# Gate blocks beside the SSD scans, the LRU branch's products beside the last GDN head, head states loaded a head ahead, adaLN row weights on ScalarE's queue

## The chip, the cores and the metric

The kernel runs on one core of one Trainium2 chip. The metric is the device time of a run in microseconds (us). The kernel before takes 3340.12 us, the median of three runs (3339.49 to 3342.93).

## What is computed

One layer of a diffusion backbone with 1024 tokens of width 1024. Only the part around the change is shown; after it come a hierarchical mixture of experts and a final norm.

```python
h_l = rmsnorm(x_l) * (1 + mod_l[1]) + mod_l[0]          # adaLN rows: mod = silu(c) @ w_mod + b_mod
parts = h_l @ w_in                                       # 93 column blocks: LRU, GDN, SSD inputs, gates
lru_l = lru_branch(...)                                  # gated linear recurrence
gdn_l = gdn_branch(...)                                  # gated DeltaNet, 8 heads, two directions
ssd_l = ssd_branch(...)                                  # Mamba-2 scan, 2 groups of 8 heads, two directions
gates = sigmoid(gate_pre).reshape(b, l, 3, 1024)
acc = 0.0
for k in range(3):
    acc = acc + gates[:, :, k] * (branches[k] @ w_branch[k])
x_l = x_l + mod_l[2] * (acc @ w_out)                     # rows mod[2..5] are made beside the merge
```

Every large product is made from fp32 operands that are split into a high and a low part, and adds three products: high by high, low by high, high by low.

## The kernel before, in words

**Blocks.** The weights of `w_in` come in 93 blocks of 128 columns. For each block `WBlocks.get` loads the raw weights with SyncE's queue (`raw<-in_w_in`), ScalarE makes the high part (`whi`), VectorE or GpSimd the low part (`wlo`), and `mmblock` issues 48 TensorE matmuls of 512 columns into a PSUM tile `pj`. The 24 products of the merge (`w_branch`) and the 8 of the output projection (`w_out`) have the same 48 matmuls. There are two `pj` tiles, so a block can start while the one before it is being read.

**Side tasks.** Everything else (convolutions, scans, norms, head chains) is written as Python generators in a list (`add`, `post`). `run` goes through a list of jobs; a job is a block or a callable. `mmblock` calls `tick` between matmul triples, and each tick moves every side task that its clock takes to be ready by one step. So the instruction order of each engine is fixed when the program is built, by the job list, the flags that tasks wait for (`wait`, `until`, `take`) and the builder's clock. Each engine then works strictly through its own order. All instructions are recorded on line 255, so they are told apart here by the names of their tiles.

**Stages.** The order of jobs is LRU (to about 640 us), the context part of GDN (to 754), SSD group 0 (blocks, then its scan to 929), SSD group 1 (blocks, then its scan to 1179), the SSD output gate blocks and norm (to 1248), eight GDN heads (to about 2050), the left-over gate blocks (to 2107), the merge (to 2422), the output projection, routing and the experts.

**Gate blocks.** 24 of the 93 blocks make the merge gates. They depend on nothing but `hl` (the split tokens), so `gate_jobs` can put them anywhere. `gate_done` turns each into two half tiles `gt` with ScalarE and stores them to DRAM (`gate`) with ScalarE's queue. The table `G` gives their places: 4 behind LRU, 6 in the GDN context part, 2, 2 and 0 behind the blocks of SSD group 0, of group 1 and of the SSD output, 1, 4 and 3 behind heads 5, 6 and 7, and the last 2 in the tail.

**The SSD scan.** `ssd_intra` works in rounds for one chunk and direction: GpSimd makes masks `gm`, TensorE sums them (`parg`), ScalarE takes the exponential (`L`), VectorE and ScalarE scale it by the head's scores (`t`), GpSimd and VectorE multiply (`L`), and TensorE applies it (`py`). `ssd_scan` carries the state `sst`: TensorE `pcs` and `pss`, VectorE `tm`, `sst` and `ya`, GpSimd `xd`. `ssd_final` does the norm and 32 transposes `pto`.

**GDN heads.** `gdn_head_ops` makes keys, queries and decays of a head; `gdn_chain` then carries two states `S` (one per direction) through eight steps, each `ch` matmuls, `w` and `S` on VectorE and scalings `k`, `ktg` on ScalarE. The start states are loaded from DRAM (`S<-sgd`) at the chain's start with ScalarE's queue. One more block per head, the output gate `GZ+h`, is kept in tile `gz`.

**Merge.** `merge` goes through the branches in the order LRU, SSD, GDN (`MERGE`), k = 0, 1, 2, and for each through eight products j. `stage_branch` and `stage` load a branch row block from DRAM (`st<-br`, two buffers) and split it into `bh` and `bl`. Each product needs its gate row back (`gt<-gate`); the first branch writes `acc`, the others add to it. At its side `mod_rows` (one generator step per tick) makes the four adaLN rows on VectorE: for each row eight loads `wr<-in_w_mod` of 512 KB, eight `macc` instructions and two `pmr` matmuls. `drain` finishes what is left of it before `out_proj`.

Of the kernel before, what the change touches and what calls it, by code (L numbers as in the profile page):

```python
# [11 lines left out]
F32 = mybir.dt.float32  # L12
# [4 lines left out]
ALU = mybir.AluOpType  # L17
# [4 lines left out]
P = 128  # L22
D = 1024
KT = D // P
SEQ = 1024
# [9 lines left out]
MERGE = (0, 2, 1)  # L35
# [102 lines left out]
ZP = 2  # L138
# [130 lines left out]
class Core:  # L269
    def __init__(self, tc, io, ctx):  # L270
        self.tc = tc
        self.clk = Clock()
        self.nc = Engines(self.clk, tc.nc)
        self.io = io
        self.ctx = ctx
        self.cnt = 0
        self.post = []
        self.flags = set()
        self.live = [0, 0]
        self.gates = 0  # L280

    def pool(self, name, bufs=1, **kw):
        return self.ctx.enter_context(self.clk.pool(self.tc, name=name, bufs=bufs, **kw))
# [152 lines left out]
    def mod_rows(self):  # L436

        nc = self.nc
        w_mod, b_mod = self.io["w_mod"], self.io["b_mod"]
        mp = self.mg  # L440
        one = mp.tile([P, 1], F32, name="one")
        nc.vector.memset(one, 1.0)

        def load(i):
            w = mp.tile([P, D], F32, tag="w", name="wr", bufs=3)
            c0 = 2048 + D * (i // KT)
            nc.sync.dma_start(out=w, in_=w_mod[i % KT * P:(i % KT + 1) * P, c0:c0 + D])
            return w
        q = deque([load(0), load(1)])
        for i in range(4 * KT):  # L450
            k = i % KT
            if i + 2 < 4 * KT:
                q.append(load(i + 2))
            w = q.popleft()
            a = self.act[:, k, 0:1]
            if k == 0:
                acc = mp.tile([P, D], F32, tag="macc", name="macc", bufs=1)
                nc.vector.tensor_scalar(out=acc, in0=w, scalar1=a, scalar2=None, op0=ALU.mult)
            else:
                nc.vector.scalar_tensor_tensor(out=acc, in0=w, scalar=a, in1=acc, op0=ALU.mult, op1=ALU.add)  # L460
            if q:
                self.clk.last = self.clk.ready[q[0].tensor.name]
            yield
            if k == KT - 1:
                r = i // KT
                b = mp.tile([1, D], F32, tag="b", name="mb")
                nc.sync.dma_start(out=b, in_=b_mod[:, 2048 + D * r:2048 + D * (r + 1)])
                for n0 in (0, 512):
                    ps = self.aux.tile([P, 512], F32, tag="aux", name="pmr")
                    nc.tensor.matmul(ps[0:1, :], lhsT=one, rhs=acc[:, n0:n0 + 512], start=True,  # L470
                                     stop=True)
                    nc.vector.tensor_tensor(out=b[:, n0:n0 + 512], in0=b[:, n0:n0 + 512], in1=ps[0:1, :], op=ALU.add)
                    yield
                nc.sync.dma_start(out=self.modrow[r:r + 1, :], in_=b)
# [991 lines left out]
    def gdn_head_ops(self, h, bts):  # L1466

        if h > 1:
            yield from self.wait(("gch", h - 2))
        yield from self.wait(("gpre", h))  # L1470
        for bt in bts:
            yield from self.gdn_keys(bt, norms=False)
        self.flags.add(("gkt", h))
        yield from self.wait(("gb", VB + h), *[("gop", 2 * h - 2, 1)] * (h > 0))
        for bt in bts:
            yield from self.gdn_values(bt)
        self.gd.used["vc"] -= 1
        yield from self.wait(*[("gi", bt.id) for bt in bts])
        for p in range(2):
            if h:  # L1480
                yield from self.wait(*([("gch", h - 1)] if p else [("gk3", h - 1)]))
            qs = [self.gd.tile([P, 4, P], F32, tag=f"qs{p}{d}", name="qs") for d in range(2)]
            e1 = self.e1d.rearrange("(t c) p -> t c p", c=16)
            for d in range(2):
                f = d if p == 0 else 1 - d
                self.nc.scalar.dma_start(out=qs[d], in_=e1[4 * f:4 * f + 4, 8 * d + h, :].unsqueeze(0).to_broadcast([P, 4, P]))
            yield
            for d in range(2):
                bt = bts[d if p == 0 else 1 - d]
# [92 lines left out]
    def gdn_chain(self, h, bts, og):  # L1582
# [2 lines left out]
        g = self.gd  # L1585
        if h > 1:
            yield from self.wait(("gch", h - 2))
        st = [g.tile([P, P], F32, tag="S", name="S") for _ in range(2)]
        for d in range(2):
            nc.scalar.dma_start(out=st[d], in_=self.sgd[h, d])  # L1590
        if h:
            yield from self.wait(("gch", h - 1))
        yield from self.wait(("gop", 2 * h, 0))
        pa, pb = self.ch
        for k in range(8):
# [80 lines left out]
    def gdn_jobs(self, n):  # L1676
# [31 lines left out]
            self.flags.add(("gpre", h))  # L1708

        def zdone(b, ps, lat):  # L1710
            if b > GZ and not LAZYZ:
                self.until(("gh", b - GZ - 1))
            self.add(zblock(b - GZ, ps))

        def zblock(h, ps):
            if h:
                yield from self.wait(("gh", h - 1))
            zs[h] = z = self.gd.tile([P, SEQ], F32, tag="gz", name="gz")
            self.nc.scalar.activation(out=z, in_=ps, func=AF.Silu)
            self.give(ps)  # L1720
            self.flags.add(("gz", h))
# [8 lines left out]
        jobs = blocks(0) + blocks(1) + self.gate_jobs(n[0])  # L1730
        for h in range(8):
            b = blocks(h + 2) if h < 6 else []
            jobs += [lambda h=h: head(h)] + b[:ZP] + [(GZ + h, "lat", zdone)] + b[ZP:]
            jobs += self.gate_jobs(n[1 + h])
        return jobs


    def split(self, hi, lo, src, scale=1.0):
# [25 lines left out]
    def merge(self, cur):  # L1764
        nc = self.nc
        mg = self.mg
        ma = self.ma
        acc = mg.tile([P, KT, SEQ], F32, tag="acc", name="acc", bufs=1)
        self.add(self.mod_rows())
        for k in range(3):  # L1770
            nx = []
            for j in range(KT):
                hi, lo = self.ws.get()
                gt = mg.tile([P, SEQ], F32, tag="gt", name="gt", bufs=2)
                nc.sync.dma_start(out=gt, in_=self.gate[8 * MERGE[k] + j])
                if k < 2 and j < 4:
                    nx.append(self.stage(mg, self.pair(ma, 12), self.br[MERGE[k + 1]][j]))
                ps = self.ppool.tile([P, SEQ], F32, tag="pj", name="pj")
                self.mmblock(ps, hi, lo, lambda i: cur[i], SEQ, self.tick, kouter=True)
                dst = acc[:, j, :] if k == 0 else gt  # L1780
                nc.vector.scalar_tensor_tensor(out=dst, in0=gt, scalar=1.0, in1=ps, op0=ALU.add, op1=ALU.mult)
                if k:
                    nc.vector.tensor_tensor(out=acc[:, j, :], in0=acc[:, j, :], in1=gt, op=ALU.add)
                if k == 2 and j < 4:
                    nx.append(self.pair(ma, 12))
                    self.split(nx[j][0], nx[j][1], acc[:, j, :], 0.5)
            for j in range(4, KT):
                if k < 2:
                    nx.append(self.stage(mg, self.pair(ma, 12), self.br[MERGE[k + 1]][j]))
                else:  # L1790
                    nx.append(self.pair(ma, 12))
                    self.split(nx[j][0], nx[j][1], acc[:, j, :], 0.5)
            cur = nx
        self.drain()
        return cur
# [488 lines left out]
def build(tc, io, out=None, stages=("lru", "ssd", "gdn", "moe"), dbg=None):  # L2284
    with ExitStack() as ctx:
        c = Core(tc, io, ctx)
        with tc.manual_schedule():
# [3 lines left out]
            c.gate = dr.tile([24, P, SEQ], F32, name="gate")  # L2291
            c.kvd = dr.tile([16, P, CTX], F32, name="kvd")
            c.e1d = dr.tile([P, P], F32, name="e1d")
            c.sgd = dr.tile([8, 2, P, P], F32, name="sgd")
            c.modrow = dr.tile([4, D], F32, name="modrow")
            c.x2d = dr.tile([SEQ, D], F32, name="x2d")
# [6 lines left out]
                dbg(c)  # L2303


G = {"mix": [0,1,2,2,2,2,2,2,2,2,2,2,2,2,1,0], "lru": 4, "gc": 6, "ssd": [2, 2, 0],
     "gdn": [0, 0, 0, 0, 0, 0, 1, 4, 3]}


def phase1(c, tc, io, stages):  # L2310
# [13 lines left out]
        J["ssd"] = c.ssd_jobs(0, G["ssd"][0]) + c.ssd_jobs(1, G["ssd"][1]) + c.gate_jobs(G["ssd"][2])  # L2324
    if "gdn" in stages:
        J["gdn"] = c.gdn_jobs(G["gdn"])
    J["tail"] = c.gate_jobs(24 - c.gates)
    order = [j for n in ("sm", "lru", "gc", "ssd", "gdn", "tail") for j in J[n] if not callable(j)]
    srcs = [io["w_in"][b] for b, _, _ in order]
    if "moe" in stages:  # L2330
# [2 lines left out]
    with c.clk.pool(tc, name="w", bufs=1, side="right") as c.wp, ExitStack() as psum, ExitStack() as right:  # L2333
        c.ppool = psum.enter_context(c.clk.pool(tc, name="pj", bufs=2, space=PSUM))
        c.aux = Banks(c, psum.enter_context(c.clk.pool(tc, name="aux", bufs=1, space=PSUM)), 4)
        with c.clk.pool(tc, name="hl", bufs=1) as hlp:
# [34 lines left out]
                c.ma = right.enter_context(c.clk.pool(tc, name="ma", bufs=1, side="right"))  # L2371
            with c.clk.pool(tc, name="gp", bufs=2) as c.gp, c.clk.pool(tc, name="st", bufs=1) as c.mg:
                cur = []
                if "moe" in stages:
                    c.add(c.stage_branch(0, cur))
                c.run(J["tail"])
                c.drain()
        if "moe" not in stages:
# [236 lines left out]
```

## Time and profile before

| what | value |
|---|---|
| median of 3 runs | 3340.12 us |
| profiled execution | 3341.23 us |
| its span | 3339.5 us |
| mean granted TensorE clock | 0.941 of full speed |
| TensorE matmuls busy | 2955.1 us, 88% |
| VectorE busy | 2141.1 us, 64% |
| ScalarE busy | 1573.0 us, 47% |
| GpSimd busy | 758.9 us, 23% |
| DMA, mean over the span | 129 GB/s |

A page of the profile gives shares over the whole span; the stages have different limits, so the views that matter here are cut to stretches of time. In them, PE is TensorE, PEld its weight loads, DVE is VectorE, ACT ScalarE, POOL GpSimd, SP SyncE, and a q behind an engine's name is its DMA queue. The granted clock is 1.00 at 2.4 GHz and falls towards 0.5 (1.2 GHz) in stretches where TensorE is throttled.

### The profile page before, as it was taken

The page shows a single profiled execution, that of the slowest core. Times are in us where ns is not written, and L with a number is a line of the kernel's source. Part 1 is how long each engine was busy: PE and PEld are TensorE (multiplying, and loading weights), DVE is VectorE, ACT ScalarE, POOL GpSimd, SP SyncE. Part 2 cuts the span into 40 slices and gives each one's busy share as a digit, 9 for nine tenths or more (in the row PEclk, how much of TensorE's full clock was granted, in tenths as well). Part 3 has the DMA queues.
Part 4 walks back from the last instruction along what each step waited for, and adds up shares of the span by engine and source line. Part 5 has one row for each costly group of instructions (what it writes and reads, how often), then busy time and mean ns, then how long its engine had stood idle before and what let it go on. Part 6 is the DMA issues. An engine that isn't in the chain of part 4 may idle for free. (4 is left out here: it accounts for less than half of the span.)

```text
span 3339.5 us, 47272 instructions
## 1 busy us (share of the span) xinstructions
PE 2955.1 (88%) x18539; PEld 2351.2 (70%) x18539; DVE 2141.1 (64%) x3730; ACT 1573.0 (47%) x2263; POOL 758.9 (23%) x642
## 2 busy tenths in 40 slices
PE   7978789989799789999999899889977899999992
PEld 3756667777478467787888777667765788878881
DVE  4677765744834836888788752244544888787785
ACT  4556564344225224455555443211122567676673
POOL 1121221203513512112021111211100233343333
PEclk9989999989799789999999999999988899999996
DMA  5112222211012011111121112455334698888895
GB/s 190 61 60 79 74 71 80 90 33 45 7 45 63 7 52 46 41 33 47 41 48 47 53 47 73 176 183 186 139 137 189 247 345 307 300 341 301 311 353 223
DMA packets 123009, 431.56 MB, mean 129 GB/s; under 512 B 18200, under 2 KB 44056, under 8 KB 97184
## 3 DMA queue, kind: packets, MB, share of 16 engines
q1 hardware_dynamic: 77712, 371.18, 31.0%
q10 hardware_dynamic: 33616, 36.34, 3.7%
q0 software_dynamic: 11456, 21.00, 1.8%
q8 instruction: 147, 2.41, 0.3%
q14 instruction: 78, 0.64, 0.1%
HBM read 389.57 MB, written 59.85 MB: 135 GB/s over the span
## 5 line engine op out<-in xcount | busy, mean ns | idle before, releaser
L255 PE MATMUL pj<-hhi,whi 128*128 128x512 f32 x1488 | 630.3, 424 | 10.1 <-DVE qT L255 5.0
L255 PE MATMUL pj<-hhi,wlo 128*128 128x512 f32 x1488 | 592.4, 398 | 3.7 <-POOL wlo L255 2.5
L255 PE MATMUL pj<-hlo,whi 128*128 128x512 f32 x1488 | 592.2, 398 | 0.0
L255 DVE TENSOR_TENSOR wl<-raw,wh 128x2048 fp32r<-128x2048 f32 x188 | 448.0, 2403 | 102.9 <-ACT wh L255 100.3
L255 POOL TENSOR_TENSOR wlo<-raw,whi 128x1024 fp32r<-128x1024 f32 x78 | 195.3, 2504 | 1027.3 <-ACT whi L255 911.5
L255 ACT ACTIVATE wh<-raw 128x2048 fp32r<-128x2048 f32 x188 | 360.6, 1918 | 128.7 <-PE psu L255 103.1
L255 PEld LDWEIGHTS pj<-hhi,wlo 128*128 128x128 f32 x1488 | 281.9, 189 | 74.1 <-POOL wlo L255 4.0
L255 PEld LDWEIGHTS pj<-hhi,whi 128*128 128x128 f32 x1488 | 283.7, 191 | 68.3 <-issue 6.8
L255 PEld LDWEIGHTS pj<-hlo,whi 128*128 128x128 f32 x1488 | 283.8, 191 | 56.3 <-issue 3.2
L255 ACT ACTIVATE whi<-raw 128x1024 fp32r<-128x1024 f32 x145 | 152.6, 1055 | 320.5 <-PE pj L255 233.0
L255 PE MATMUL psu<-wl,xh 128*128 128x512 f32 x576 | 227.4, 395 | 2.9 <-DVE wl L255 2.9
L255 PE MATMUL psu<-wh,xh 128*128 128x512 f32 x576 | 228.1, 396 | 0.0
L255 PE MATMUL psu<-wh,xl 128*128 128x512 f32 x576 | 226.1, 392 | 1.3 <-DVE xl L255 1.3
L255 DVE TENSOR_TENSOR wlo<-raw,whi 128x1024 fp32r<-128x1024 f32 x67 | 85.5, 1276 | 206.1 <-ACT whi L255 205.4
L255 ACT ACT_TABLE_LOAD x127 | 162.9, 1283 | 82.0 <-DVE xt L255 28.0
L255 POOL TENSOR_TENSOR yo<-yo,m 128x1024 f32<-128x1024 f32 x35 | 103.6, 2959 | 183.2 <-ACT yo L255 183.1
L255 PE MATMUL psg<-u,lw 128*128 128x512 f32 (+1 forms) x192 | 88.6, 598 | 56.2 <-issue 53.4
L255 PE MATMUL pj<-bh,whi 128*128 128x512 f32 x384 | 122.8, 401 | 14.6 <-DVE acc L255 8.7
L255 PEld LDWEIGHTS psu<-wl,xh 128*128 128x128 f32 x576 | 108.8, 189 | 29.8 <-DVE wl L255 8.3
L255 PE MATMUL pj<-bl,whi 128*128 128x512 f32 x384 | 122.1, 400 | 8.3 <-POOL bl L255 5.9
L255 PEld LDWEIGHTS psu<-wh,xl 128*128 128x128 f32 x576 | 108.7, 189 | 24.1 <-DVE xl L255 2.1
L255 PEld LDWEIGHTS psu<-wh,xh 128*128 128x128 f32 x576 | 109.2, 190 | 22.5 <-ACT xh L255 0.2
(472 smaller groups left out, 6189.0 us busy)
## 6 DMA issues: line engine op xcount, KB each, us to landing
raw<-in_w SPq DMA_DIRECT2D x188, 1024.0 KB, 7.4
raw<-in_w_in SPq DMA_DIRECT2D x119, 512.0 KB, 3.6
wr<-in_w_mod SPq DMA_DIRECT2D x32, 512.0 KB, 6.2
gate<-gt ACTq DMA_DIRECT2D x48, 256.0 KB, 2.0
raw<-in_w_branch SPq DMA_DIRECT2D x24, 512.0 KB, 3.6
st<-br SPq DMA_DIRECT2D x24, 512.0 KB, 4.8
gt<-gate SPq DMA_DIRECT2D x24, 512.0 KB, 5.0
wm<-in_w_mod SPq DMA_DIRECT2D x8, 1024.0 KB, 5.8
```

The costliest lines, as they stand in the source:

```text
L255: return f(*args, **kw)
```

## The change

It does five things. Ten gate blocks are put into the SSD stage (5, 4 and 1 in place of 2, 2 and 0), two each behind heads 5 and 6, none behind head 7 and none in the tail. The eight products of the merge's first branch leave the merge loop: six are made beside the chain of head 7 (`merge_jobs`, with operands that `merge_stage` writes over `hl`), two in the tail; each is scaled by its gate and stored to DRAM (`m0d`), and the merge loads the eight results into `acc` before its 16 remaining products. The block `GZ+7` stands before head 7 and uses a tile of tag `vc`. The states `S` are loaded by `gdn_head_ops` with SyncE's queue, one head ahead. And `mod_rows` issues its loads with ScalarE's queue in place of SyncE's.

```diff
@@ mod_rows
-            nc.sync.dma_start(out=w, in_=w_mod[i % KT * P:(i % KT + 1) * P, c0:c0 + D])
+            nc.scalar.dma_start(out=w, in_=w_mod[i % KT * P:(i % KT + 1) * P, c0:c0 + D])
@@ gdn_head_ops
+        bts[0].t["S"] = st = [self.gd.tile([P, P], F32, tag="S", name="S") for _ in range(2)]
+        for d in range(2):
+            self.nc.sync.dma_start(out=st[d], in_=self.sgd[h, d])
+        self.flags.add(("gs0", h))
         yield from self.wait(("gpre", h))
@@ gdn_chain
-        st = [g.tile([P, P], F32, tag="S", name="S") for _ in range(2)]
-        for d in range(2):
-            nc.scalar.dma_start(out=st[d], in_=self.sgd[h, d])
-        if h:
-            yield from self.wait(("gch", h - 1))
+        yield from self.wait(("gs0", h), *[("gch", h - 1)] * (h > 0))
+        st = bts[0].t["S"]
@@ gdn_jobs
-            if h:
+            if h == 7:
+                yield from self.take(self.gd, "vc")
+            elif h:
                 yield from self.wait(("gh", h - 1))
-            zs[h] = z = self.gd.tile([P, SEQ], F32, tag="gz", name="gz")
+            zs[h] = z = self.gd.tile([P, SEQ], F32, tag="vc" if h == 7 else "gz", name="gz")
...
+            if h == 6:
+                jobs.append(lambda: self.add(self.merge_stage(self.gd, "k")))
             jobs += self.gate_jobs(n[1 + h])
+            if h == 6:
+                jobs += [(GZ + 7, "lat", zdone), lambda: self.flags.add("hl"), lambda: head(7)]
+                jobs += self.merge_jobs(NM0, lambda: (self.gd, "k"))
+    def merge_stage(self, pool, tag):
+        def load(b):
+            raw = pool.tile([P, SEQ], F32, tag=tag, name="st")
+            self.nc.sync.dma_start(out=raw, in_=self.br[MERGE[0]][b])
+            return raw
+        yield from self.wait(("gkt", 7))
+        raw = [load(0), load(1)]
+        yield from self.wait("hl")
+        for b in range(KT):
+            self.split(self.hl[0][:, b, :], self.hl[1][:, b, :], raw[b])
+            if b + 2 < KT:
+                raw.append(load(b + 2))
+            self.flags.add(("mst", b))
+            yield
+        self.flags.add("mst")
+
+    def merge_jobs(self, n, where):
+        def job(j):
+            def rhs(i):
+                self.until(("mst", i))
+                return self.hl[0][:, i, :], self.hl[1][:, i, :]
+            hi, lo = self.ws.get()
+            while self.live[True] == 2:
+                self.tick(True)
+            self.live[True] += 1
+            ps = self.ppool.tile([P, SEQ], F32, tag="pj", name="pj")
+            self.mmblock(ps, hi, lo, rhs, SEQ, self.tick, kouter=not j)
+            self.add(done(j, ps))
+
+        def done(j, ps):
+            yield from self.wait("mst")
+            pool, tag = where()
+            gt = pool.tile([P, SEQ], F32, tag=tag, name="gt")
+            self.nc.sync.dma_start(out=gt, in_=self.gate[8 * MERGE[0] + j])
+            yield
+            self.nc.vector.scalar_tensor_tensor(out=gt, in0=gt, scalar=1.0, in1=ps, op0=ALU.add, op1=ALU.mult)
+            self.give(ps)
+            self.nc.sync.dma_start(out=self.m0[j], in_=gt)
+            yield
...
@@ merge
         self.add(self.mod_rows())
-        for k in range(3):
+        for j in range(KT):
+            nc.sync.dma_start(out=acc[:, j, :], in_=self.m0[j])
+        for k in range(1, 3):
...
-G = {..., "lru": 4, "gc": 6, "ssd": [2, 2, 0],
-     "gdn": [0, 0, 0, 0, 0, 0, 1, 4, 3]}
+G = {..., "lru": 4, "gc": 6, "ssd": [5, 4, 1],
+     "gdn": [0, 0, 0, 0, 0, 0, 2, 2, 0]}
+NM0 = 6
@@ phase1
-    J["tail"] = c.gate_jobs(24 - c.gates)
+    J["tail"] = c.merge_jobs(KT - c.merged, lambda: (c.mg, "gt"))
...
-                    c.add(c.stage_branch(0, cur))
+                c.add(c.stage_branch(1, cur))
```

TensorE does the same matmuls in both kernels, in another order.

**TensorE in the scan of SSD group 0.** Before, the second round of the scan stands alone; these rows follow the last block of the group:

```order
L255 MATMUL pcb<-cT,bT 128x128
L255 MATMUL pcs<-sst_178,cT 128x512
L255 MATMUL pcb<-cT,bT 128x128
L255 MATMUL pcs<-sst_179,cT 128x512
L255 MATMUL parg<-gm,mr 128x512 x4
L255 MATMUL pss<-xd,bt 128x512
L255 MATMUL parg<-gm,mr 128x512 x4
```

In the change the matmul triples of the added gate blocks stand between them:

```order
L255 MATMUL pcs<-sst_179,cT 128x512
L255 MATMUL pj<-hhi,whi 128x512
L255 MATMUL pj<-hlo,whi 128x512
L255 MATMUL pj<-hhi,wlo 128x512
L255 MATMUL parg<-gm,mr 128x512 x4
L255 MATMUL pcb<-cT,bT 128x128
L255 MATMUL pss<-xd,bt 128x512
L255 MATMUL pcs<-sst_180,cT 128x512
```

Three blocks that stood outside the scan of group 0 are spread over its rounds in this way, and two over those of group 1; the last four or five steps of each scan, which have no `parg`, still stand without blocks.

**SyncE's queue at the start of the merge.** Before, it loads the first branch and then one weight, one gate row, one row of the next branch and some `wr` per product:

```order
L255 DMA st<-br_77 128x1024
L255 DMA raw<-in_w_branch 128x1024
L255 DMA st<-br_77 128x1024 x7
L255 DMA raw<-in_w_branch 128x1024
L255 DMA gt<-gate 128x1024
L255 DMA st<-br_79 128x1024
L255 DMA wr<-in_w_mod 128x1024 x3
```

In the change these rows stand around the last products of the first branch and the first of the second:

```order
L255 DMA raw<-in_w_branch 128x1024
L255 DMA gt<-gate 128x1024
L255 DMA st<-br_79 128x1024
L255 DMA m0d<-gt 128x1024
L255 DMA gt<-gate 128x1024
L255 DMA st<-br_79 128x1024
L255 DMA m0d<-gt 128x1024
L255 DMA st<-br_79 128x1024 x4
L255 DMA acc<-m0d 128x1024 x8
L255 DMA raw<-in_w_branch 128x1024
L255 DMA gt<-gate 128x1024
L255 DMA st<-br_78 128x1024
```

The `wr` loads are gone from this queue, and the stores `m0d`, which wait for VectorE, and the eight loads of `acc` stand in it ahead of the rows of the second branch and of the weights.

**VectorE at the end of the merge.** Before, the last adaLN row is done some products earlier:

```order
L255 TENSOR_TENSOR mb<-mb,pmr 1x512
L255 SCALAR_TENSOR_TENSOR gt<-gt,pj 128x1024
L255 TENSOR_TENSOR acc<-acc,gt 128x1024
L255 SCALAR_TENSOR_TENSOR gt<-gt,pj 128x1024
L255 TENSOR_TENSOR acc<-acc,gt 128x1024
L255 TENSOR_TENSOR wlo<-raw,whi 128x1024
L255 SCALAR_TENSOR_TENSOR gt<-gt,pj 128x1024
L255 TENSOR_TENSOR acc<-acc,gt 128x1024
L255 SCALAR_TENSOR_TENSOR bl<-acc,bh 128x1024 x4
```

In the change it stands behind the last product:

```order
L255 SCALAR_TENSOR_TENSOR gt<-gt,pj 128x1024
L255 TENSOR_TENSOR acc<-acc,gt 128x1024
L255 SCALAR_TENSOR_TENSOR bl<-acc,bh 128x1024 x4
L255 TENSOR_TENSOR mb<-mb,pmr 1x512 x2
L255 TENSOR_SCALAR macc<-wr,act 128x1024
L255 SCALAR_TENSOR_TENSOR macc<-wr,act,macc 128x1024 x7
L255 TENSOR_TENSOR mb<-mb,pmr 1x512 x2
L255 TENSOR_TENSOR bl<-st,bh 128x1024 x4
```

The whole last row of `mod_rows` has moved behind the merge, where `drain` issues it before the output projection; on ScalarE's queue six of its eight loads stand ahead of the split of the next `w_out` weights.

## Rows read from the trace of the kernel before

**Rows 1.** The page, busy time of each engine: TensorE.
```profile
PE 2955.1 (88%) x18539; PEld 2351.2 (70%) x18539; DVE 2141.1 (64%) x3730; ACT 1573.0 (47%) x2263; POOL 758.9 (23%) x642
```

**Rows 2.** Stretches: length, busy PE, PEld, DVE, ACT, POOL (instructions); clock, DMA share, GB/s.
```profile
815.00:840.00 25.00, 24.43 (x120) 19.04 (x119) 20.17 (x41) 13.88 (x34) 15.07 (x20) 1.00 0.13 43
840.00:929.00 89.00, 63.92 (x198) 37.80 (x197) 72.41 (x122) 19.63 (x53) 49.98 (x59) 0.78 0.04 12
851.00:874.00 23.00, 17.10 (x60) 11.37 (x60) 17.71 (x34) 6.57 (x20) 14.51 (x20) 0.72 0.00 0
904.00:929.00 25.00, 18.10 (x41) 6.83 (x41) 24.00 (x34) 0.00 (x0) 10.75 (x7) 0.98 0.07 21
1092.00:1179.00 87.00, 63.39 (x197) 36.82 (x197) 71.84 (x121) 19.37 (x53) 49.14 (x58) 0.77 0.04 13
1228.00:1248.00 20.00, 9.23 (x43) 7.32 (x44) 6.68 (x13) 15.34 (x27) 0.00 (x0) 0.66 0.16 66
...
2049.00:2107.00 58.00, 58.00 (x263) 47.03 (x262) 7.39 (x14) 16.85 (x22) 9.61 (x4) 1.00 0.30 106
2107.00:2159.00 52.00, 40.17 (x148) 28.41 (x147) 14.94 (x12) 13.46 (x14) 14.37 (x6) 0.93 0.53 190
2159.00:2423.00 264.00, 245.88 (x1028) 190.67 (x1027) 124.53 (x96) 43.25 (x42) 41.51 (x17) 0.98 0.47 169
2423.00:2456.00 33.00, 18.11 (x51) 11.64 (x50) 13.54 (x10) 8.36 (x8) 8.14 (x3) 0.74 0.50 166
```

**Rows 3.** The same view for tile pj alone (block matmuls; no column for POOL).
```profile
815.00:840.00 25.00, 13.21 (x48) 8.66 (x48) 0.00 (x0) 1.20 (x2) 1.00 0.13 43
...
2015.00:2049.00 34.00, 15.50 (x50) 8.56 (x49) 0.00 (x0) 1.21 (x2) 0.95 0.12 39
2049.00:2107.00 58.00, 56.32 (x239) 44.16 (x238) 0.00 (x0) 5.79 (x9) 1.00 0.30 106
...
2159.00:2423.00 264.00, 237.87 (x1012) 189.99 (x1011) 26.05 (x22) 0.00 (x0) 0.98 0.47 169
```

**Rows 4.** Timeline of PE in the scan: start, length, instruction, [idle before <-releaser].
```profile
850.88 6.40 PE L255 MATMUL py<-xs,L 128*128 128x128 f32 x32 [2.89 <-POOL L L255]
...
898.04 6.70 PE L255 MATMUL py<-xs,L 128*128 128x128 f32 x32 [3.65 <-POOL L L255]
```

**Rows 5.** Timelines of DVE and POOL near 921 us, beside a block's low-part split.
```profile
921.07 0.68 DVE L255 TENSOR_TENSOR sst<-sst,pss 128x512 f32<-128x512 f32 x1
921.66 2.24 DVE L255 TENSOR_TENSOR ya<-ya,tm 128x512 f32<-128x512 f32 x1
...
920.56 2.79 POOL L255 TENSOR_TENSOR wlo<-raw,whi 128x1024 fp32r<-128x1024 f32 x1
```

**Rows 6.** Timelines of ACT, its queue and PE at the starts of two chains.
```profile
1908.06 0.91 ACTq L255 DMA_DIRECT2D S<-sgd  x2
1909.02 0.69 ACT L255 ACTIVATE k<-kt,ge 128x128 f32<-128x128 f32 x2
...
1915.64 1.22 PE L255 MATMUL ch<-S,WT 128*128 128x128 f32 x4 [9.58 <-DMA S<-sgd]
...
2020.47 1.22 PE L255 MATMUL ch<-S,WT 128*128 128x128 f32 x4 [4.86 <-DMA S<-sgd]
```

**Rows 7.** Timeline of SyncE's queue at the first products of the merge.
```profile
2103.85 20.89 SPq L255 DMA_DIRECT2D st<-br  x7
...
2158.09 11.00 SPq L255 DMA_DIRECT2D wr<-in_w_mod  x2
```

**Rows 8.** DMA issues of 2150 to 2400 us: KB each, median us to landing.
```profile
wr<-in_w_mod SPq DMA_DIRECT2D x27, 512.0 KB, 6.2
...
gt<-gate SPq DMA_DIRECT2D x20, 512.0 KB, 5.5
```

**Rows 9.** Groups of 2107 to 2423 us: busy us, mean ns | idle before <-releasers.
```profile
L255 DVE SCALAR_TENSOR_TENSOR macc<-wr,act,macc 128x1024 f32<-128x1024 f32 x28 | 44.3, 1584 | 10.1 <-DMA wr<-in_w_mod 9.6
...
L255 ACT ACTIVATE bh<-st 128x1024 fp32r<-128x1024 f32 x23 | 24.4, 1060 | 143.7 <-DMA st<-br 143.3 <-ACT gt L255 0.4
```

More of the change, by code (lines that the diff above doesn't have):

```diff
@@ L279, in __init__ @@
         self.live = [0, 0]
-        self.gates = 0
+        self.gates = self.merged = 0
     def pool(self, name, bufs=1, **kw):
@@ L1710, in zdone @@
         def zdone(b, ps, lat):
-            if b > GZ and not LAZYZ:
+            if GZ < b < GZ + 7:
                 self.until(("gh", b - GZ - 1))
@@ L1732, in gdn_jobs @@
             b = blocks(h + 2) if h < 6 else []
-            jobs += [lambda h=h: head(h)] + b[:ZP] + [(GZ + h, "lat", zdone)] + b[ZP:]
+            jobs += [lambda h=h: head(h)] * (h < 7) + b[:ZP] + [(GZ + h, "lat", zdone)] * (h < 7) + b[ZP:]
+            if h == 6:
+                jobs.append(lambda: self.add(self.merge_stage(self.gd, "k")))
             jobs += self.gate_jobs(n[1 + h])
-        return jobs
+            if h == 6:
+                jobs += [(GZ + 7, "lat", zdone), lambda: self.flags.add("hl"), lambda: head(7)]
+                jobs += self.merge_jobs(NM0, lambda: (self.gd, "k"))
+        return jobs
+    def merge_stage(self, pool, tag):
[35 more added lines that the diff above has]
+            yield
+        a = self.merged
+        self.merged += n
+        return [lambda j=j: job(j) for j in range(a, a + n)]
     def split(self, hi, lo, src, scale=1.0):
@@ L1779, in merge @@
                 self.mmblock(ps, hi, lo, lambda i: cur[i], SEQ, self.tick, kouter=True)
[L1780 to L1783, printed above, removed]
+                nc.vector.scalar_tensor_tensor(out=gt, in0=gt, scalar=1.0, in1=ps, op0=ALU.add, op1=ALU.mult)
+                nc.vector.tensor_tensor(out=acc[:, j, :], in0=acc[:, j, :], in1=gt, op=ALU.add)
                 if k == 2 and j < 4:
@@ L2293, in build @@
             c.e1d = dr.tile([P, P], F32, name="e1d")
+            c.m0 = dr.tile([KT, P, SEQ], F32, name="m0d")
             c.sgd = dr.tile([8, 2, P, P], F32, name="sgd")
@@ L2303, in build @@
                 dbg(c)
-G = {"mix": [0,1,2,2,2,2,2,2,2,2,2,2,2,2,1,0], "lru": 4, "gc": 6, "ssd": [2, 2, 0],
-     "gdn": [0, 0, 0, 0, 0, 0, 1, 4, 3]}
+G = {"mix": [0,1,2,2,2,2,2,2,2,2,2,2,2,2,1,0], "lru": 4, "gc": 6, "ssd": [5, 4, 1],
+     "gdn": [0, 0, 0, 0, 0, 0, 2, 2, 0]}
+NM0 = 6
 def phase1(c, tc, io, stages):
@@ L2326, in phase1 @@
         J["gdn"] = c.gdn_jobs(G["gdn"])
-    J["tail"] = c.gate_jobs(24 - c.gates)
+    assert c.gates == 24
+    J["tail"] = c.merge_jobs(KT - c.merged, lambda: (c.mg, "gt"))
     order = [j for n in ("sm", "lru", "gc", "ssd", "gdn", "tail") for j in J[n] if not callable(j)]
@@ L2373, in phase1 @@
                 cur = []
-                if "moe" in stages:
-                    c.add(c.stage_branch(0, cur))
+                c.add(c.stage_branch(1, cur))
                 c.run(J["tail"])
```

## The prediction

> **What bounds the kernel now.** I read the busy shares first: TensorE works 88% of the span [rows 1], and the change leaves its matmuls as they are. So only its idle time and its slow time can be won, and the next view is the one by stretches, which shows where these are. Three places matter. In the scans of the SSD groups (89 and 87 us) TensorE is busy about 63 us each, at a granted clock of 0.78 and 0.77 [rows 2], and the scan's last `py` and the one two rounds before it lie 47.2 us apart, with waits for GpSimd's `L` ahead of them [rows 4]: a round takes 23.6 us and its length is set by the loop over VectorE and GpSimd. In the end of the SSD stage (1228 to 1248) TensorE is busy 9.2 of 20 us. And around the merge it waits for operands: 40.2 of 52 us busy for the first three products, 18.1 of 33 in the entry to the output projection [rows 2]. The remaining stretch, 2049 to 2107, is full: five gate blocks, 239 block matmuls in 58 us, nearly all of it busy [rows 2, 3]. It gains nothing by being faster; it can only go elsewhere.
>
> **How the sum is made.** I count by marks in the profiled execution (3341.23 us, span 3339.5, 1.1 above the median). The heads 0 to 6 have the same number of blocks in both kernels: behind heads 5 and 6 one gate fewer, and `GZ+7` more. Six gate blocks more stand in the SSD stage, and what stood beside and behind head 7's chain is gone from there.
>
> **Removed.** From 2015 to 2107, in 34 + 58 = 92 us, lie `GZ+7` (50 block matmuls beside the chain) and five gate blocks [rows 3]. All six are now done earlier. That is −92 us, the one big term, and it is sure as far as the six blocks cost little in their new places and the chain finds other work beside it; both follow as terms.
>
> **SSD stage: +16 us.** A block is 48 matmuls of 512 columns; in the steady merge 1012 of them take 237.9 us [rows 3], 0.235 each, so a block is 11.3 us. In a round without a block TensorE works 17.1 of 23 us at a clock of 0.72 [rows 2], which is 12.3 us at full speed. 12.3 + 11.3 = 23.6: one block fills one round exactly. The block that already lies in the first round shows it: from 815 to 840 its 48 matmuls and 72 of the scan take 25 us, with TensorE busy 24.4 at full clock [rows 2, 3]; the scan alone does 60 in 23. So a block in a round costs between nothing and what is delayed when TensorE is full. Group 0 gets three blocks over about three rounds: 3 to 18 us, I take 10, nearer the middle because VectorE is nearly as full (72 of 89 us, and 24 of 25 in the last steps [rows 2]). Group 1 gets two, with one round that holds about 1.35: 0.35 × 11.3 = 4 us (0 to 9). The last one falls into the 20 us of the output norm, of which 10.8 are idle: 2 us (0 to 4). One GpSimd split beside the scan costs VectorE 2.24 instead of 0.68 us for an instruction that meets it, 1.6 us [rows 5]; two such splits, some 3 us, are in the 10 + 4. The Trainium skill (SBUF — State Buffer, the section on SBUF's two separate sides) says that GpSimd and VectorE share a port pair as an exclusive lock for a whole instruction. By that rule each split could hold VectorE for all its 2.79 us, 5.6 instead of 3 for two, and the sum would be 2 to 3 us higher; the one row here shows a part of that.
>
> **Head states: −8 us.** TensorE stands 9.6 and 4.9 us for `S`, whose loads were issued on ScalarE's queue a few us before [rows 6]. With the load a head ahead these waits end at the next latest thing: ScalarE's scaling `k` at 1909.0 to 1909.7, so about 6 of the first wait go, and of the second 1 to 3, where `k` follows the loads as closely. I take −8 (−3 to −12), since the clock also drops in such holes. The two loads go to SyncE's queue, where a 64 KB load ahead of 512 KB ones costs nothing that shows.
>
> **Chain and products: +6 us.** Before, 24 products take 52 + 264 = 316 us [rows 2]. Now: the chain of head 7 with product 0 beside it, 35 us (34 with one block before [rows 3]). Products 1 to 7 have operands and weights long ready: 7 × 11.3 = 79. Then the first three of the second branch. Before, the first branch was staged late: seven `st` loads took 20.9 us of SyncE's queue [rows 7], and three products took 52. In the change the `st` rows of the second branch stand in that queue behind the `m0d` stores, which wait for VectorE, and eight `acc` loads (4 MB) stand ahead of the next weights and gate rows. At best this hides beside products 6 and 7 (34 us), at worst it adds a landing of a gate row of 5.5 [rows 8] twice to the 52 (63). I take 52 again. The remaining 13 products: 264 us for 21.1 of them before, 12.5 each [rows 2, 3]. SyncE's queue then also held `wr` issues that waited up to 11.0 us for a buffer, ahead of the next weights [rows 7]; with them on ScalarE's queue I take 12.0, halfway to the 11.3 of full speed, 156 us. The danger is named below: ScalarE's own splits stand behind these waits now. In sum 35 + 79 + 52 + 156 = 322, against 316.
>
> **Entry to the output projection: +19 us.** `mod_rows` moves a step per tick, and 16 products give fewer ticks than 24. Its last row, eight `macc` of 1.27 us or more (mean 1.58 [rows 9]) with loads of 6.2 us [rows 8] and three buffers, now stands behind the last product. With two loads in and six to come, each about (6.2 + 1.3) / 3 = 2.5 us after the other, that is 15 us, and the `pmr` matmuls and the split of the `w_out` weights behind it some 4. VectorE is free of other work there, so nothing hides it: 33 us become 52. Bounds: 5, if the loads run ahead and half of the 8 × 1.27 = 10 us lies in the 15 us that the old entry stood idle anyway; and 30, if only two loads are under way at a time (3 × 7.5, and 8 behind it).
>
> **Sum.** −92 + 16 − 8 + 6 + 19 = −59: 3341.2 − 59 = 3282 us. ±0.2% is ±6.7 us, about what a measurement of this kernel can tell from no change.
>
> **Rivals.**
> 1. *The moved loads buy nothing.* The Trainium skill (DMA: Bandwidth & Descriptors, the section "Issuing engines are not separate DMA queues") says that transfers of all issuing engines run on the same 16 DMA engines. Without the gain in pitch the 13 products stay at 12.5: +7, 3289 us. The wait of `wr` issues in SyncE's queue [rows 7] speaks against it, the DMA share of 0.47 [rows 2] neither way. Chance 0.10.
> 2. *ScalarE's queue becomes the wait.* A `wr` load waits for a `macc` before it on VectorE, and ScalarE's `bh` and `whi` splits stand behind it. If each of 13 products loses 2.5 to 3 us by that, about half of a landing of 6.2 us [rows 8]: +33 to 40, 3315 to 3322 us. For it: 11 us long waits of `wr` before [rows 7]. Against: ScalarE is busy 43 of 264 us there [rows 2], and its `bh` instructions wait 143 us for `st` as it is [rows 9]. Chance 0.12.
> 3. *Blocks in the scan are only half hidden.* Five times 5.6 is 28 instead of 14, and with it the late staging (63) or the long entry (30) that go with a VectorE running late: +25 to +36, 3307 to 3318. For it: VectorE at 24 of 25 us [rows 2]. Chance 0.08.
> 4. *Slower: the scan's hops queue behind triples.* TensorE works in order. If a hop (`pcs`, `pss`, `parg`, `py`) is ready while three block matmuls (0.7 us) stand ahead of it, eight times in a round, and nothing is hidden, a block costs 11.3 + 5.6 = 16.9 us: five make 84 and the last 2, 86 instead of 16, 3352 us. It decides the sign when a round with a block takes over about 39 us, for the rest of the change is worth 75, 15 per block. Against: 815 to 840 with a block in it was no longer than a round alone [rows 2, 3]. Chance 0.03.
> 5. *Better.* Products and staging run at full speed: 13 at 11.3 (−9) and the first three hidden partly (−8 to −11): 3262 to 3266. Chance 0.09.
> 6. *The states come early but the chain still waits.* If it is `k`, behind `gt` and `whi` on ScalarE, that ends last, the −8 go: 3290. Chance 0.04.
>
> **How the numbers follow.** The forecast has 0.54; with its bounds (not all at one end) it spans 3266 to 3302. The range of 3260 to 3314 takes in rivals 1 and 6, most of 5 and about half of 2 and 3; outside lie some 0.17. Faster by over 0.2% has 0.94: all but rival 4 and the upper ends of 2 and 3 coming together, 0.03 for no change, 0.03 for slower.
>
> **What would show it.** Rounds of the SSD scans at 22 to 27 us and a granted clock near 1.0 in them; the scan of group 1 ending about 14 us later than before, near 1193; no TensorE idle of over 3 us ahead of `ch<-S,WT`; no stretch of gate blocks behind head 7; products 1 to 7 at 11.3 us; `pmr` and `macc` in a gap of some 50 us behind the last product. The forecast is wrong if rounds take over 35 us, if ScalarE's splits wait for its own `wr` issues in most products, or if the entry to the output projection is as short as before.

## The result, and the profile after

| | median us | range, runs | ratio to before, 95% interval |
|---|---|---|---|
| before | 3339.8 | 3336.1 to 3342.9, 4 | |
| the change | 3298.93 | 3295.62 to 3303.31, 4 | 0.9877 (0.9865 to 0.9890) |

The change is 41 us faster where 58 were forecast. The time lies in the range of 3260 to 3314, 17 us above the point. The profiled execution took 3298.6 us, its span is 3296.9. These lines of the page answer to [rows 1] and to the clock of 0.941:

```profile
span 3296.9 us, 47286 instructions
PE 2918.7 (89%) x18539; PEld 2331.5 (71%) x18539; DVE 2144.6 (65%) x3734; ACT 1569.8 (48%) x2260; POOL 756.0 (23%) x638
```

TensorE has as many instructions as before and is busy 36 us less, and the mean granted clock is 0.954 instead of 0.941: more of them ran at the upper level. Where the time went is read from the view by stretches of the changed kernel (length, busy PE, PEld, DVE, ACT, POOL; clock, DMA share, GB/s), against [rows 2]:

```profile
840.00:905.00 65.00, 61.33 (x284) 47.68 (x284) 48.20 (x80) 22.38 (x54) 46.14 (x53) 0.97 0.15 49
905.00:934.00 29.00, 20.89 (x55) 9.24 (x53) 24.55 (x39) 3.90 (x8) 10.22 (x8) 0.94 0.05 18
1099.00:1136.00 37.00, 34.57 (x161) 27.09 (x160) 28.64 (x48) 13.28 (x31) 23.09 (x30) 1.00 0.17 57
1136.00:1190.00 54.00, 39.27 (x132) 21.82 (x131) 42.81 (x72) 11.03 (x29) 26.66 (x29) 0.87 0.03 11
1250.00:1259.00 9.00, 5.89 (x34) 3.63 (x32) 4.42 (x8) 8.18 (x11) 0.00 (x0) 1.00 0.45 177
2001.00:2021.00 20.00, 15.96 (x86) 13.23 (x85) 3.17 (x6) 10.80 (x26) 1.62 (x1) 1.00 0.28 80
2021.00:2067.00 46.00, 29.77 (x177) 23.59 (x177) 19.31 (x44) 17.81 (x31) 13.84 (x20) 1.00 0.24 80
2067.00:2148.00 81.00, 79.02 (x342) 63.20 (x340) 19.69 (x22) 10.28 (x11) 7.21 (x3) 1.00 0.43 156
2148.00:2210.00 62.00, 43.55 (x145) 32.02 (x146) 18.37 (x15) 10.37 (x10) 11.88 (x5) 0.81 0.63 227
2210.00:2365.00 155.00, 148.55 (x633) 117.73 (x631) 85.75 (x65) 26.68 (x26) 22.24 (x9) 0.99 0.55 188
2365.00:2414.00 49.00, 20.70 (x58) 10.57 (x58) 24.87 (x22) 8.47 (x8) 7.96 (x3) 0.76 0.48 160
```

In order: the scan of SSD group 0 with its three blocks in it is nearly full at a clock of 0.97, and only its last steps (905 to 934) still leave TensorE idle. In the scan of group 1 the 37 us with its two blocks are full, the 54 behind them are not (busy 39.3, clock 0.87). The norm leaves 9 us where it left 20. `GZ+7` takes 20 us, the chain of head 7 with product 0 takes 46, products 1 to 7 take 81. The first three products of the second branch take 62 us, busy 44 of them; the other 13 take 155; and the entry to the output projection takes 49, busy 21. TensorE has idle time in three stretches behind 2021; what they cost against the old merge, which had idle time too, the experiments show.

### The profile page after: what moved, and what is told of

Its sections match the earlier page's. It is cut to its first block, busy times and chain, and to the rows that moved or that the text cites. A ratio compares the mean times of both kernels' runs of the same rounds, so it can differ in the third digit from the quotient of the medians.

```text
span 3296.9 us, 47286 instructions
## 1 busy us (share of the span) xinstructions
PE 2918.7 (89%) x18539; PEld 2331.5 (71%) x18539; DVE 2144.6 (65%) x3734; ACT 1569.8 (48%) x2260; POOL 756.0 (23%) x638
## 5 line engine op out<-in xcount | busy, mean ns | idle before, releaser
L255 PE MATMUL pj<-hhi,whi 128*128 128x512 f32 x1616 | 680.4, 422 | 16.9 <-ACT hhi L255 6.8
L255 PE MATMUL pj<-hhi,wlo 128*128 128x512 f32 x1616 | 640.2, 397 | 6.9 <-POOL wlo L255 3.7
L255 PE MATMUL pj<-hlo,whi 128*128 128x512 f32 x1616 | 640.5, 397 | 6.5 <-DVE hlo L255 4.8
L255 PEld LDWEIGHTS pj<-hhi,whi 128*128 128x128 f32 x1616 | 306.1, 190 | 82.6 <-issue 8.4
L255 PEld LDWEIGHTS pj<-hhi,wlo 128*128 128x128 f32 x1616 | 304.8, 189 | 83.3 <-POOL wlo L255 5.3
L255 PEld LDWEIGHTS pj<-hlo,whi 128*128 128x128 f32 x1616 | 306.2, 190 | 72.1 <-DVE hlo L255 7.0
L255 PEld LDWEIGHTS psu<-wh,xl 128*128 128x128 f32 x576 | 108.7, 189 | 23.6 <-DVE xl L255 1.7
L255 PE MATMUL psy<-wh,xh 128*128 128x512 f32 x288 | 117.5, 408 | 0.7 <-ACT xh L255 0.7
L255 PE MATMUL psy<-wh,xl 128*128 128x512 f32 x288 | 114.6, 398 | 0.2 <-DVE xl L255 0.2
```

Source lines behind the costliest of these rows:

```text
L255: return f(*args, **kw)
```

## The experiments

Each kernel was timed beside runs of the kernel before; the median of those was 3340.1, 3336.8 and 3337.2 in the three groups, so kernels of different groups are compared by their ratios.

### The gate blocks alone

```diff
 G = {..., "lru": 4, "gc": 6,
-     "ssd": [2, 2, 0], "gdn": [0, 0, 0, 0, 0, 0, 1, 4, 3]}
+     "ssd": [5, 4, 1], "gdn": [0, 0, 0, 0, 0, 0, 2, 2, 0]}
```

> The kernel before with only the places of the gate blocks changed (5, 4 and 1 in the SSD stage, two each behind heads 5 and 6, none behind head 7 or in the tail); the merge stays as it was. Theory (the blocks are hidden in the scans, as the trace after shows with the SSD stage 12 us longer): +12 for the stage, -58.6 for the five gate blocks behind head 7, +5 to +10 since the first branch is then staged with no block beside it: 3298 to 3306 us, so most of the whole gain. Rival (the gain of the change came from the products beside head 7, and gate blocks in the scan only change places with idle time elsewhere): 3320 or more.

Measured: 3299.0 us, ratio 0.9874 (0.9858 to 0.9889). The theory holds: two lists of the table give as much as the whole change. The two waits of the chains for `S` are still there, in the waits of TensorE of this kernel from 1900 to 2060:

```profile
PE ch L255 <- DMA S<-sgd: 12.8, 2, 8.5
```

### The head states alone, and their queue alone

```diff
 # gdn_head_ops, a head ahead (as in the change)
+        bts[0].t["S"] = st = [...]
+            self.nc.sync.dma_start(out=st[d], in_=self.sgd[h, d])
```

> The kernel before with only the head states loaded a head ahead on SyncE's queue. Theory: the 9.6 and 4.9 us waits ahead of the chains' first matmuls shrink to what the scaling k sets, -5 to -8 us: 3332 to 3335. Rival (ScalarE's k ends last in any case): within 2 us of before.

Measured: 3317.8 us, ratio 0.9932 (0.9917 to 0.9946), −22 us: three times what the theory gave. The waits for `S` are gone whole; they were 14.4 us [rows 6]. Most of the gain lies there: from the first block of the heads to the first `ch` of head 7's chain, with 36 blocks between, it is 772.9 us before (first row, to 2020.47 [rows 6]), 757.1 with the states alone (next two rows) and 759.1 in the whole change (last two):

```profile
1247.60 0.48 PE L255 MATMUL pj<-hhi,whi 128*128 128x512 f32 x1
1245.20 0.48 PE L255 MATMUL pj<-hhi,whi 128*128 128x512 f32 x1
2002.34 0.60 PE L255 MATMUL ch<-S,WT 128*128 128x128 f32 x4
1259.17 0.53 PE L255 MATMUL pj<-hhi,whi 128*128 128x512 f32 x1
2018.24 0.60 PE L255 MATMUL ch<-S,WT 128*128 128x128 f32 x4
```

The order that the builder writes has moved too: on TensorE the chain of head 5 begins 0.9 blocks earlier, that of head 6 half a block later, and the eight steps of head 7 are spread over 1.6 blocks instead of 1.1. From the first block of the heads to the last gate block, 42 blocks, it takes 841 us:

```profile
1245.00:2002.00 757.00, 716.58 (x7611) 607.54 (x7612) 579.33 (x1746) 387.63 (x777) 125.13 (x210) 0.99 0.17 48
2002.00:2086.00 84.00, 83.38 (x424) 68.24 (x423) 19.09 (x50) 26.03 (x45) 16.84 (x21) 1.00 0.25 89
```

Before, these were 767 us and, as [rows 2, 3] show, 34 + 58 = 92 us, 18 more in sum; now TensorE is busy 83.4 of 84 in the second. What the moved order gives apart from the waits was not tried alone.

The other half of that edit is the queue. This kernel keeps the place and changes the queue alone:

```diff
 # gdn_chain, at the chain's start
-            nc.scalar.dma_start(out=st[d], in_=self.sgd[h, d])
+            nc.sync.dma_start(out=st[d], in_=self.sgd[h, d])
```

> The kernel before with the head states loaded at the same place as before, but issued by SyncE instead of ScalarE; the orders of TensorE and VectorE stay exactly as they were. Theory (the loads took about 7 us instead of their usual 2.0 because they stood behind a gate's two stores in ScalarE's queue): the waits of 9.6 and 4.9 us go nearly whole, -8 to -14: 3323 to 3330; what is left of the 22 us of the run with the early loads comes from the earlier start of the chains in TensorE's order. Rival (only loading a head ahead helps): within 3 us of before.

Measured: 3342.4 us, ratio 1.0013 (1.0003 to 1.0022). The theory falls. At this place the loads stand in SyncE's queue behind a weight load that waits for its buffer, and are issued later than before (1910.1 and 2022.3 instead of 1908.1 [rows 6] and 2018.1). Timelines of SyncE's queue and of TensorE:

```profile
1909.74 0.33 SPq L255 DMA_DIRECT2D raw<-in_w_in  x1
1910.12 0.90 SPq L255 DMA_DIRECT2D S<-sgd  x2
...
2006.73 15.52 SPq L255 DMA_DIRECT2D raw<-in_w_in  x2
2022.31 0.89 SPq L255 DMA_DIRECT2D S<-sgd  x2
...
1915.80 1.22 PE L255 MATMUL ch<-S,WT 128*128 128x128 f32 x4 [10.38 <-DMA S<-sgd]
```

So the queue alone does not take the wait away; the place a head ahead, on SyncE's queue, does. A load a head ahead on ScalarE's queue was not tried.

### Both, with the merge as it was

This kernel has the edits of the first two experiments and nothing else of the change.

> The kernel before with two parts of the change: the places of the gate blocks and the head states loaded a head ahead; the merge stays as it was. Theory (the two are gains in different stages, 41 us and 22 us alone, and the rest of the change, which makes the first branch beside head 7, costs about 20): 3276 to 3284 us, faster than the whole change. Rival (both fill the same idle time at head 7, so they overlap and the rest costs nothing): 3293 to 3300.

Measured: 3275.3 us, ratio 0.9821 (0.9806 to 0.9836). The two gains add up (0.9874 × 0.9932 = 0.9807), and the kernel beats the whole change: the rest of it (the early products, `GZ+7` ahead of head 7, the `wr` queue) costs 0.9877 / 0.9821, 0.6% or some 19 us, and the two intervals do not meet. Stretches of this kernel: the chain of head 7 with `GZ+7` beside it, the 24 products, the entry to the output projection:

```profile
1998.00:2047.00 49.00, 34.74 (x220) 30.11 (x219) 19.22 (x52) 21.02 (x50) 4.89 (x14) 0.91 0.21 63
2047.00:2361.00 314.00, 287.93 (x1168) 220.61 (x1169) 140.60 (x108) 55.29 (x54) 56.27 (x23) 0.96 0.48 171
2361.00:2393.00 32.00, 17.67 (x49) 11.35 (x48) 14.03 (x10) 8.36 (x8) 8.14 (x3) 0.74 0.48 162
```

49 + 314 = 363 us for `GZ+7`, the chain and 24 products; the change needs 20 + 46 + 81 + 62 + 155 = 364 for the same. Making eight products early thus came out even, and the entry, 49 instead of 32, is the loss.

### The queue of the adaLN weights, twice

The changed kernel with `nc.sync` in `mod_rows` again:

> The changed kernel with the adaLN row weights back on SyncE's queue. Theory of the forecast (the wr issues on SyncE's queue delay the next weights): the 13 later products at 12.5 instead of 11.9, +6 to +8 us: 3305 to 3307. Rival (the queue that issues them does not matter, as the Trainium skill has it): within 3 us of the change. A gain would mean that ScalarE's splits wait behind wr issues.

Measured: 3300.8 us, ratio 0.9889 (0.9874 to 0.9905): the same as the change. The other way round, gates and states with `nc.scalar` in `mod_rows`:

> The run with gates and states, with the adaLN row weights on ScalarE's queue, as in the change: the only part of the change that has not been tried in a merge of 24 products. Theory from the forecast: the later products go from 12.5 towards 11.9 us, -5 to -10: 3265 to 3270. Rival, as the run with the loads back on SyncE's queue bore it out: within 3 us of 3275. A loss would say that ScalarE's splits wait behind wr issues.

Measured: 3278.5 us, ratio 0.9822 (0.9809 to 0.9836): the same as without. The queue that issues these loads does not matter here, as the Trainium skill has it (DMA: Bandwidth & Descriptors, "Issuing engines are not separate DMA queues"). With the loads on SyncE's queue the 13 products of the changed kernel take 156 us, against 155:

```profile
2215.00:2371.00 156.00, 149.70 (x634) 118.58 (x633) 85.73 (x66) 26.83 (x26) 21.98 (x9) 0.98 0.52 187
```

Nor is there a faster pitch to explain. The last 13 products took as long before the change (first row) and take as long with gates and states alone (second row), both with `wr` on SyncE's queue, some 11.8 us each:

```profile
2269.00:2423.00 154.00, 148.97 (x638) 117.34 (x638) 77.01 (x61) 26.82 (x26) 22.14 (x9) 1.00 0.44 156
2206.00:2361.00 155.00, 149.10 (x638) 117.45 (x637) 77.57 (x61) 26.83 (x26) 22.48 (x9) 1.00 0.45 163
```

### Product 0 beside the chain

```diff
-                jobs += [..., lambda: head(7)]
+                jobs += [..., lambda: head(7), lambda: self.until(("gch", 7))]
```

> The changed kernel with one wait more in the order of the jobs: the products of the first branch start only when head 7's chain has been issued, so the chain has no matmuls of product 0 between its own. Theory (product 0's operands are split just in time, and TensorE, in order, holds the chain for them: 46 us for chain and product 0 where 35 were forecast): chain 29 to 32 us, then eight products at 11.2: 119 to 122 in place of 127.6, 3290 to 3293 us. Rival (the chain is slow by its own hops, whatever stands between): chain 40 or more, then 90: 3301 or slower.

Measured: 3296.4 us, ratio 0.9875 (0.9857 to 0.9893): no difference from the change. Both forecasts are half right. The chain alone takes 29 us, as the theory said, but product 0 then takes 20 by itself, 49 for what took 46:

```profile
2017.00:2046.00 29.00, 19.24 (x135) 16.52 (x134) 16.59 (x43) 13.47 (x27) 6.73 (x15) 0.98 0.22 73
2046.00:2066.00 20.00, 15.46 (x55) 11.04 (x55) 7.54 (x10) 6.86 (x8) 7.10 (x3) 0.84 0.29 105
```

In the change TensorE holds the chain for operands (first rows below), and the six later operand loads leave SyncE's queue over 33 us, because two buffers come free only when the splits that stand between the chain's steps are done. Timelines of PE and SyncE's queue of the change:

```profile
2030.13 0.73 PE L255 MATMUL pj<-hhi,whi 128*128 128x512 f32 x2 [1.42 <-ACT hhi L255]
2032.57 0.74 PE L255 MATMUL pj<-hlo,whi 128*128 128x512 f32 x2 [1.71 <-POOL hlo L255]
...
2022.85 33.30 SPq L255 DMA_DIRECT2D st<-br  x6
```

So this staging has to end before product 0 can, whether TensorE waits inside the chain or behind it. What more buffers would give was not tried.

### The m0d stores out of SyncE's queue

```diff
-            self.nc.sync.dma_start(out=self.m0[j], in_=gt)
+            (self.nc.gpsimd if j > 5 else self.nc.sync).dma_start(out=self.m0[j], in_=gt)
```

> The changed kernel with the last two m0d stores issued by GpSimd instead of SyncE, so that the loads of the second branch no longer stand behind a store that waits for VectorE. Theory (this order makes the first three products of the second branch take 61 us): 8 to 10 us less there, 3288 to 3291. Rival (two staging buffers of 512 KB set the pace whatever stands ahead): within 3 us of the change.

Measured: 3292.3 us, ratio 0.9870 (0.9853 to 0.9887). By the ratios that is some 2 us below the change, and the intervals overlap, so by time alone it is not settled. The trace bears the theory out in part: 8 to 10 us less were expected, and the first three products of the second branch take 56 us instead of 62. In the change the queue runs

```profile
2159.56 0.32 SPq L255 DMA_DIRECT2D m0d<-gt  x1
2159.98 9.55 SPq L255 DMA_DIRECT2D st<-br  x4
2169.58 5.04 SPq L255 DMA_DIRECT2D acc<-m0d  x8
```

and without the store in it

```profile
2152.78 12.65 SPq L255 DMA_DIRECT2D st<-br  x5
2165.53 5.57 SPq L255 DMA_DIRECT2D acc<-m0d  x8
```

The last `st` leaves 4 us earlier. The rest of the 56 us (three products at full speed are 34) is not taken apart; the rival's staging through two buffers, which also stood before the change [rows 7], fits it.

### The last adaLN row before the last product

```diff
-            w = mp.tile([P, D], F32, tag="w", name="wr", bufs=3)
+            w = mp.tile([P, D], F32, tag="w", name="wr", bufs=4)
...
-        q = deque([load(0), load(1)])
+        q = deque([load(0), load(1), load(2)])
...
-            yield
+            if k % 3 != 1:
+                yield
             if k == KT - 1:
```

> The changed kernel with the adaLN rows made faster: a generator step more in some ticks and a fourth load buffer, so that the last row is done before the last product. Theory (the last row stands alone between the last product and the output projection, 21 us of TensorE's idle time): entry from 48.8 to about 31, 3279 to 3284 us. Rival (the entry is set by the staging of the w_out rows, or the instructions put among the products delay these as much): 3293 or more.

Measured: 3306.8 us, ratio 0.9900 (0.9884 to 0.9917), slower than the change by some 8 us. The entry behaved as the theory said: 49 us became 32. In the change TensorE stood 21 us there for the last row:

```profile
2387.89 3.57 PE L255 MATMUL pmr<-macc,one 128*1 128x512 f32 x4 [20.95 <-DVE macc L255]
```

But the same 13 products took 178 us instead of 155:

```profile
2218.00:2396.00 178.00, 160.75 (x643) 121.86 (x642) 99.50 (x78) 27.04 (x26) 22.18 (x9) 0.93 0.51 179
```

The next run asked whether that is ScalarE's queue; it is the kernel above with `nc.sync`:

> As the run in which the adaLN rows were made faster, with their loads on SyncE's queue. There the entry fell from 48.8 to 32.8 us as expected, but the products before it took 24 us more. Theory (ScalarE's queue: splits bh and whi stand behind wr issues that wait for macc, three per product now): most of the 24 comes back, 3282 to 3290. Rival (the row store modrow on SyncE's queue, which waits for pmr, holds the loads of the next branch behind it, on whichever queue wr is): 3303 or more.

Measured: 3308.6 us, ratio 0.9913 (0.9898 to 0.9927); the queue is not the cause. Neither is the rival's store the main one: TensorE's waits for operands of the products come to some 4 us in these 13 products, as in the change. Its waits for `macc` grew, in the change, in the run with faster rows and in the one with the loads on SyncE's queue:

```profile
PE pmr L255 <- DVE macc L255: 2.8, 1, 2.8
```

```profile
PE pmr L255 <- DVE macc L255: 13.7, 3, 5.4
```

```profile
PE pmr L255 <- DVE macc L255: 14.8, 3, 5.8
```

TensorE takes its instructions in order, so a `pmr` that comes before its `macc` is done holds the products behind it. The builder wrote the rows denser than VectorE, in its own order, got to them; in the run with faster rows VectorE never stood idle for a load ahead of a `macc` of this stretch. So 21 us at the end became 14 in the midst, 11 more than in the change, and with a clock of 0.93 instead of 0.99 TensorE was busy 12 us longer over that stretch. Together that is the 23 us. A place for the row that costs nothing was not found.

### One gate block more behind the heads

Two kernels take one gate block of head 6 away again, from gates and states; the first sets `"gdn": [..., 2, 1, 1]`, the second `[..., 2, 1, 0]`, which leaves one for the tail.

> The run with gates and states, with one gate block moved from behind head 6 to behind head 7. Theory (between head 7's chain and the first product of the merge TensorE has one block of work in 48 us, so a block there is mostly free, while the stretch of head 6 gets shorter by a block): 5 to 10 us faster than 3275, 3265 to 3270. Rival (its triples lengthen the chain as much): 3273 to 3278.

Measured: 3273.7 us, ratio 0.9810 (0.9796 to 0.9823): not to be told from 0.9821, the rival's case; the 5 to 10 us of the theory did not come. Its median is the lowest of this study, but not clear of the run it was made from.

> The run with gates and states, with one gate block moved from behind head 6 to the tail, where the first branch is staged. Theory (it covers the staging, so that the first two products take 11 to 12 us instead of 23.6 and 14.8, but not the end of head 7's chain): 3 to 8 us faster than 3275. Rival (the drain ahead of the tail is what costs): 3275 or slower.

Measured: 3281.3 us, ratio 0.9829 (0.9816 to 0.9843): no gain, the rival's case.

## Why the prediction came out as it did

The terms by the marks of the two traces (starts of the same matmuls on TensorE):

| step of the forecast | forecast | measured |
|---|---|---|
| six blocks gone from the stretch 2015 to 2107 | −92 | −92 |
| SSD stage | +16 | +12 |
| head states | −8 | −5 in the stretch of the heads, whose mark lies ahead of the second wait |
| chain of head 7 and 24 products | +6 | +29 |
| entry to the output projection | +19 | +16 |
| rest | 0 | −2 |
| sum | −59 | −42 |

**Right: the blocks in the scans.** The one large gain and its price hold. The rounds with blocks in them are full at clocks of 0.97 and 1.00, the heads start at 1259 instead of 1248, and the run with the gates alone shows that this part by itself is worth 41 us. One reading was a little too kind: the round with a block before the change took 25 us, which is not "no longer" than the 23.6 of a round alone. Rivals 3 and 4 are out (28 and 86 us against 12), and with the queue's two runs rival 2, whose loss did not come. Rival 5 is out too: the first three products of the second branch took 62 us.

**Right: the entry.** 49 us against 52 forecast, with TensorE waiting 21 us for the last row's `macc` ahead of `pmr`. The six loads to come leave ScalarE's queue over 14.5 us, where the sum had 15:

```profile
2367.77 14.50 ACTq L255 DMA_DIRECT2D wr<-in_w_mod  x6
```

**Wrong: "The chain of head 7 with product 0 beside it, 35 us."** It took 46. The forecast took 34 us from a stretch in which the block beside the chain had its operands ready [rows 3]; product 0 gets its operands by splits that stand between the chain's own steps. Letting it wait until the chain was over changed nothing, so it is the staging that takes the time.

**Wrong in size: the first three products of the second branch.** 52 was taken from before, between 34 and 63; it was 62. The mechanism named has a part in it: the rows stand behind the `m0d` stores, and with the last two stores gone from the queue it was 56. The other 4 us are not taken apart.

**Right by luck: 13 products at 12.0.** They took 11.9, but not because the `wr` loads had left SyncE's queue. The step that failed is the 12.5 for them before: it is the mean of 21 products, of which the first eight took 110 us (2159 to 2269) and the last 13 took 154, 11.8 each. The wait of 11.0 us in the queue [rows 7] stands at 2158, at the start of those eight, not among the 13. Rival 1's mechanism is true; its +7 was priced by the same mean and did not come.

**Wrong in size: the head states.** The limit of 8 us came from the thought that `k` on ScalarE would end last. The waits went whole, both of them, 14.4 us, and no wait of `ch` for `k` over 0.7 us is left, so rival 6 is out. Up to the first `ch` of head 7's chain this is 14 us in the whole change too (773 to 759) and 16 alone. The table's −5 (36 blocks, from 1247.6 to 2014.7 before and from 1259.2 to 2020.9 now) is smaller because its mark of before lies ahead of the second wait and that of now behind the chain's first `ch`; the rest of the gain is in the other rows. Alone the edit gives 22 us; what stands beyond the waits was not taken apart.

What the forecast did not see is that its parts differ in sign. By sum it was a gain with one weak term; by experiment two edits are worth 61 us together (0.9821), and the early products, with `GZ+7` ahead of head 7, cost 19, nearly all of it in the entry that the shorter merge left uncovered (49 us instead of 32).

## What to carry to other kernels

Work without dependencies can go where TensorE waits in a loop of other engines, and a round of that loop was priced here by its work at full speed plus one block against its length: for the SSD stage that sum was 4 us off. A mean over a stretch hides that its parts differ: a pitch should be taken from the very products that it is used for. Products moved into a hole bring their staging with them, and a hole is only worth what operands are ready for it; and when a stretch is shortened, ask which background task used it as cover, since it will stand bare at the stretch's end. A change of several edits should be timed edit by edit: here two small edits without the rest beat the whole.

## What the runs showed of the hardware that was not expected

A load of 64 KB landed 2.0 us after its issue in most heads (median, ScalarE's queue) and 3.8 us when SyncE's queue issued it at the same place. Ahead of head 6's chain TensorE began only 6.7 us after the second of them (1908.97 to 1915.64 [rows 6]), and still 4.8 us after it on SyncE's queue, behind a weight load of 512 KB (1911.02 to 1915.80). The two gate stores of 256 KB ahead in ScalarE's queue do not explain this by themselves. Ahead of head 7's chain two such stores stand there as well, 1.5 and 0.5 us before the loads, and these landed after 2.1 us:

```profile
2016.60 0.34 ACTq L255 DMA_DIRECT2D gate<-gt  x1
2017.61 0.34 ACTq L255 DMA_DIRECT2D gate<-gt  x1
```

What differs is two loads `qs<-e1d` of 256 KB on ScalarE's queue. For head 6 they were issued 5.4 us before the loads of `S` (1902.63) and took 11.0 us to land, until about 1914; for head 7 they were issued 14 us before (2004.04):

```profile
qs<-e1d ACTq DMA_DIRECT2D x2, 256.0 KB, 11.0
2004.04 1.04 ACTq L255 DMA_DIRECT2D qs<-e1d  x2
```

No run moved these loads, so that they are the cause is not shown. Changing the queue did not bring the 2.0 back; loading early hid it.
